# First tiles of a hybrid encoder trunk: order of fills, the inverse-root row read from its PSUM bank, no GpSimd in the first normalisation, one power op issued early

## The chip, the cores and the metric

The kernel runs on one core of a Trainium2 chip. The metric is the device time of one execution in microseconds. A core has five instruction queues, which each run their own list in order: PE (matrix multiplies), DVE (vector), ACT (scalar, activation functions), POOL (GpSimd) and SP, which here only issues DMA transfers. They wait for each other through semaphores, so an instruction that waits holds up everything behind it in its own queue.

## The reference

One layer of a hybrid streaming encoder is applied to a prompt of 2048 tokens and to a sample of 32 tokens, width 1024, all in float32. Cut to what matters here:

```
mod = (silu(c) @ ada_w + ada_b)            # 6 x 1024: shift, scale, gate of two norms
sh1, sc1, gt1, sh2, sc2, gt2 = split(mod)
h = rmsnorm(x) * g * (1 + sc1) + sh1       # rmsnorm(x) = x * rsqrt(mean(x*x) + 1e-6)
p = h @ w_in                               # u, v, q, k, v', z, a, b
a_out = u * (W_s rmsnorm(v) + b_s)         # spatial gating over 128 positions
b_out = rmsnorm(gated_delta_rule(q, k, v', a, b)) * silu(z)
x = x + gt1 * (concat(a_out, b_out) @ w_out)
h = rmsnorm(x) * g2 * (1 + sc2) + sh2
x = x + gt2 * (relu(h @ w_up)**2 @ w_down)
y = rmsnorm(x)
```

Besides `y`, the last convolution rows, the final delta-rule states and the normalised `v` rows of the sample are returned.

## The kernel before

Activations are held with the 1024 channels on partitions, as eight tiles `k` = 0 to 7 of 128 channels, and tokens along the free dimension. Tokens are worked in two halves (1024 and 1056), each cut into groups of 512, or of 384, 384 and 288. Every large product is split in three to keep float32 accuracy: operands are held as a high part and a remainder, `BH`/`BL` for activations and `wh`/`wl` for weights, and PE runs high x high, high x low, low x high. The high part is a copy on ACT, the remainder a subtraction on DVE.

The stages are: `startup` (first statistics, the first modulation and the first projection `z`, up to some 60 us), the mixers (`v_stage`, the delta rule and the `u_stage` of each half, to some 1014 us), and the feed-forward part to the end.

`startup` loads the eight tiles of group 0 (`load(0)`, names `s_477` to `s_480`, two tiles in each: `s_477` holds k = 0 and 1, `s_478` holds 2 and 3, and so on). ACT squares them, DVE adds the squares into `row[0]` (`s_493`), and `rms_row` sums over the partitions with PE (bank `M`, four columns), scales on DVE (`rcol`), raises to the power -1/2 on POOL (`tt` with `pow`, exponent `mhalf`), and spreads the result back over all partitions with four PE transposes into another bank `M`; ACT then copies that bank into `row[0]`. In between, `ada_first(k)` computes shift and scale of tile k: two loads of 512 KB (`ada`, four buffers `s_469` to `s_472`, SP waits for a free one), eight small PE products into a bank `C`, an ACT copy, two transposes back into that bank, four DVE additions into `modc` and one scaling (`a`). `h_tile` then makes the activation tile: `h_value` multiplies x by the row of inverse roots (on POOL where k % 3 == 2, so k = 2 and 5, otherwise on DVE), applies scale and shift (on POOL for k = 1 and 5, ACT for 3 and 7, DVE for the others), and `split` makes `BH[k]` and `BL[k]`. Twelve products follow for each k: four heads of `z`, three each, into three banks `g` and one bank `L`.

Group 1 of the first half takes the same way behind it (`load(1)`, `stats(1)`, with the additions alternating between DVE and POOL), while PE goes on to `v_stage`. `consts` loads constants and fills zeros on POOL: the delta-rule state, padding, and buffers whose upper part must be zero.

No queue order is written by hand. Each helper records its instruction in `Program` with an engine, an estimated cost and its predecessors; `Program.schedule` then plays the whole list through a model of the five engines (costs, latencies between engines, a shared port of DVE and POOL) and emits every queue in the order of the modelled starts. So an edit at the beginning can change the order everywhere behind it. The semaphore waits are set afterwards from the data that the instructions touch.

The helpers' lines: L351 `act`, L366 `tt`, L371 `stt`, L380 `ts`, L389 `cp`, L393 `fill`, L404 `dma`, L412 `mms` (all matrix products), L423 `tr` (transposes).

Of the kernel before, what the change touches and what calls it, by code (L numbers as in the profile page):

```python
# [11 lines left out]
ALU = mybir.AluOpType  # L12
# [31 lines left out]
PE, DVE, ACT, POOL, DMA, NONE = range(6)  # L44
# [23 lines left out]
def segs(hf, g):  # L68
    o, w = GROUPS[hf][g]
    if hf == 1 and g == 2:  # L70
        return [(0, w - NS, 0), (w - NS, NS, 1)]
    return [(0, w, 0)]
# [52 lines left out]
class View:  # L125
# [52 lines left out]
    def bc(self, shape):  # L178
        return self.step("broadcast_to", np.broadcast_to(np.uint8(0), shape), self.reg, list(shape))
# [15 lines left out]
def R(x):  # L195
    return x.ap if isinstance(x, View) else x
# [140 lines left out]
class Kern:  # L337
# [50 lines left out]
        e = self._e(eng)  # L388
        self.p.op(eng, c, lambda: e.tensor_copy(R(out), R(in_)), [out], [in_])  # L389

    def fill(self, out, value, eng=POOL):
        e = self._e(eng)
        self.p.op(eng, 100 + out.n, lambda: e.memset(R(out), value), [out], [])  # L393

    def transpose32(self, out, in_):
        nc = self.nc
# [261 lines left out]
    def startup(self):  # L658
        i, c = self.i, self.dma
        c(self.craw, i["cT"])  # L660
        self.act(self.cs, self.craw, AF.Silu)
        self.fill(self.ones, 1.0, DVE)
        self.fill(self.mhalf, -0.5, DVE)
        xr = [[8, 9, 10, 11], [4, 5, 7, 12]]
        x = [[self.slot(s, lo, (P, 512)) for s in xr[g] for lo in (0, HALF)] for g in range(2)]
        load = lambda g: [c(x[g][k], self.x_src(0)(k, 512 * g, 512)) for k in range(KT)]
        row = [self.row[:, 512 * g : 512 * g + 512] for g in range(2)]

        def stats(g):
            acc = row[g]  # L670
            self.act(acc, x[g][0], AF.Square)
            for k in range(1, KT):
                sq = self.half("E")
                self.act(sq, x[g][k], AF.Square)
                self.tt(acc, acc, sq, ALU.add, DVE if g == 0 or k % 2 else POOL)
            self.rms_row([acc], 512, acc)

        load(0)
        k1 = self.slot(13, 512, (P, 248))
        c(k1, i["k1"])  # L680
        self.adab = k1[:, :96].re("p (j k q) -> p j k q", j=6, k=KT)
        self.cp(self.nrm, k1[:, 96:120].re("p (n k) -> p n k", n=3))
        self.cp(self.ident, k1[:, 120:248])
        stats(0)
        self.sq = self.slab_list()
        self.sn = self.slab(*self.sq.pop(0))
        z = [self.next_slab(), self.sn]
        ps = [self.bank("C") for _ in range(2)]
        for e in range(2):
            self.fill(ps[e], 0.0, DVE)  # L690
        zs = [self.bank(t) for t in "gggL"]
        for k in range(KT):
            self.ada_first(k, ps[k % 2])
            self.h_tile(0, 0, k, x[0][k], row[0], self.a1, 0)
            for h in range(H):
                self.gemm_k(zs[h][:, :512], *z[h // 2], h % 2, 0, 0, k)
        for h in range(H):
            self.z_out(0, 0, h, zs[h])
        load(1)
        stats(1)  # L700
        for k in range(KT):
            self.h_tile(0, 1, k, x[1][k], row[1], self.a1, 0)
        self.next_slab()
        self.consts()

    def consts(self):
        i = self.i
        ld = lambda v, src: self.dma(v, src, 4 * int(np.prod(v.shape)))
        bc = lambda v, n: self.dma(v, i[n].partition_broadcast(P))
        with self.p.at(GEMM):  # L710
            ld(self.wsT, i["wsT"])
            self.fill(self.wsT[64:128, :, 0:64], 0.0)
            bc(self.sgub, "sgub")
            bc(self.sgug, "sgug")
            ld(self.triu, i["triu"])
            ld(self.mask, i["mask"])
            ld(self.convw, i["convw"])
            ld(self.sconv, i["sconv"])
            ld(self.dngc, i["dngc"])
            bc(self.dtb, "dtb")  # L720
            bc(self.alog, "alog")
            for h in range(H):
                self.fill(self.S[h], 0.0)
            self.fill(self.halo, 0.0)
            self.fill(self.ab, 0.0)
            zero = self.slot(4, 0, (P, 1024))[:36]
            self.fill(zero, 0.0)
            for d in self.ud_d:
                self.dma(d.re("c a x -> (c a) x"), zero)
            self.fill(self.z0, 0.0)  # L730

            for x in self.r1s + self.vns + self.ofs:
                self.fill(x, 0.0)
            zero = self.slot(4, 0, (P, 384))
            self.fill(zero, 0.0)
            for h in range(H):
                self.dma(self.us_d[h][1][:, 1024:], zero[:, :P])
                self.dma(self.pk_d[h][8][:, :, :P], zero.re("p (a b) -> p a b", a=3))
# [113 lines left out]
        self.tt(bl, x, bh.f32(), ALU.subtract, eng)  # L852

    def h_value(self, hf, g, k, x, r, a, kind):
        self.tt(x, x, r, ALU.mult, POOL if k % 3 == 2 else DVE)
        for so, sw, q in segs(hf, g):
            s = slice(so, so + sw)
            c, b = a[:, k, q : q + 1], self.modc[:, kind, k, q : q + 1]
            if k % 4 == 1 and not kind:
                self.ts(x[:, s], x[:, s], c, ALU.mult, b, ALU.add, POOL)  # L860
            elif kind or k % 4 == 3:
                self.act(x[:, s], x[:, s], AF.Identity, scale=c, bias=b)
            else:
                self.ts(x[:, s], x[:, s], c, ALU.mult, b, ALU.add)
# [1032 lines left out]
```

## Time and profile before

| what | value |
|---|---|
| median of 3 runs | 2337.24 us (2336.88 to 2339.47) |
| the profiled execution, its own time | 2330.84 us |
| its span | 2328.8 us |
| granted PE clock, mean | 0.998 |
| PE busy | 2292.2 us, 98% |
| DVE busy | 1653.2 us, 71% |
| ACT busy | 1226.1 us, 53% |
| POOL busy | 607.5 us, 26% |
| moved by DMA | 552.59 MB, 237 GB/s mean |

PE is busy nearly all the time, and its busy time is made of pipelined products. So what matters is where PE is not busy: 16.1 us of that lie in the first 60 us, 9.4 us in the last 25 us, and 11.0 us in the 2244 us between. A row of the timeline gives start, duration, engine, line, operation, output<-inputs, and in brackets the idle time before it with what ended it; of a row with xN, the start is that of the first and the duration that of all N together.

### The profile page before, as it was taken

How to read it: one execution, taken by the hardware profiler on the slowest of the kernel's cores; microseconds unless marked ns; L12 is line 12 of the kernel's file. 1: busy time of each engine (PE TensorE's matmuls, PEld its weight loads, DVE VectorE, ACT ScalarE, POOL GpSimd, SP SyncE). 2: the span in 40 equal slices, each digit the busy share in tenths (PEclk: the TensorE clock that was granted, in tenths of full speed). 3: DMA queues.
4: the chain of work that ended last, by engine and by line, in shares of the span. 5: the costliest groups of instructions: out<-in, count | busy, mean ns of one | idle time of the engine just before them, and what ended most of it. 6: DMA issues, size and time to landing. Idle time of an engine off the chain costs nothing.

```text
span 2328.8 us, 45703 instructions
## 1 busy us (share of the span) xinstructions
PE 2292.2 (98%) x15906; PEld 2171.0 (93%) x15906; DVE 1653.2 (71%) x3651; ACT 1226.1 (53%) x2816; POOL 607.5 (26%) x830
## 2 busy tenths in 40 slices
PE   7999999999999999999999999999999999999998
PEld 4877879999999888999999999999999999999998
DVE  5557646667655546589999989776668886666775
ACT  5465546666655435376556555753344564334343
POOL 2235331332423323345544424200000250000001
PEclk9999999999999999999999999999999999999999
DMA  9789666657557767888777786997667797666771
GB/s 322 224 291 317 222 183 214 188 166 232 165 157 225 242 204 232 262 290 277 248 255 251 256 280 229 344 321 233 221 214 252 264 302 232 221 214 215 246 225 54
DMA packets 367247, 552.59 MB, mean 237 GB/s; under 512 B 70988, under 2 KB 191200, under 8 KB 367016
## 3 DMA queue, kind: packets, MB, share of 16 engines
q1 hardware_dynamic: 367016, 549.68, 72.5%
q8 instruction: 125, 2.05, 0.4%
q14 instruction: 106, 0.87, 0.1%
HBM read 395.25 MB, written 154.28 MB: 236 GB/s over the span
## 4 chain that ended last, share of the span: by engine, by line
PE 59%; DMA 3%; DVE 2%; issue 1%; ACT 1%; POOL 0%; SPq 0%; POOLq 0%; DVEq 0%; ACTq 0%
PE f L412 52%; PE g L412 6%; DMA s<-th_d 1%; PE C L412 1%; DVE s L366 1%; DVE s L371 1%; ACT s L351 0%; DVE BL L366 0%; DMA wh<-sd_d 0%; DVE wl L366 0%; POOL s L366 0%; DMA wr<-w_o 0%; PE B L412 0%; DMA th_d<-s 0%; ACT BH L351 0%
## 5 line engine op out<-in xcount | busy, mean ns | idle before, releaser
L351 ACT ACTIVATE s<-s 128x348 fp32r<-128x348 f32 (+13 forms) x1077 | 496.0, 483 | 341.3 <-DVE s L366 131.4
L412 PE MATMUL f<-s,wh 128*128 128x348 f32 (+1 forms) x2768 | 662.4, 322 | 0.4 <-DVE s L366 0.3
L412 PEld LDWEIGHTS f<-s,wh 128*128 128x128 f32 x2768 | 481.0, 188 | 2.2 <-DVE s L366 1.9
L366 DVE TENSOR_TENSOR s<-f,s 128x348 f32<-128x348 f32 (+1 forms) x696 | 349.6, 515 | 170.4 <-PE f L412 169.2
L412 PE MATMUL f<-s,wl 128*128 128x348 f32 (+1 forms) x1384 | 444.9, 321 | 0.0
L412 PE MATMUL g<-BH,wh 128*128 128x512 f32 (+2 forms) x1112 | 411.3, 370 | 0.0
L412 PE MATMUL g<-BH,wl 128*128 128x512 f32 (+2 forms) x1112 | 391.4, 352 | 0.0
L412 PE MATMUL g<-BL,wh 128*128 128x512 f32 (+2 forms) x1112 | 390.1, 351 | 0.0
L366 DVE TENSOR_TENSOR s<-s,s 128x348 fp32r<-128x348 f32 (+7 forms) x679 | 350.9, 546 | 45.7 <-POOL s L366 16.7
L412 PE MATMUL f<-BL,wh 128*128 128x348 f32 (+1 forms) x1024 | 330.2, 322 | 0.0
L412 PE MATMUL f<-BH,wh 128*128 128x348 f32 (+1 forms) x1024 | 329.3, 322 | 0.0
L412 PE MATMUL f<-BH,wl 128*128 128x348 f32 (+1 forms) x1024 | 328.7, 321 | 0.0
L351 ACT ACTIVATE wh<-s 128x512 fp32r<-128x512 f32 (+1 forms) x277 | 173.7, 634 | 232.0 <-PE f L412 190.6
L366 POOL TENSOR_TENSOR s<-s,s 128x512 f32<-128x512 f32 (+5 forms) x156 | 197.6, 1275 | 330.5 <-ACT s L351 163.4
L366 POOL TENSOR_TENSOR s<-s 64x39 f32<-64x39 f32 (+12 forms) x298 | 159.5, 535 | 444.0 <-issue 381.7
L412 PEld LDWEIGHTS f<-s,wl 128*128 128x128 f32 x1384 | 260.6, 188 | 0.0
L366 DVE TENSOR_TENSOR wl<-s,wh 128x512 fp32r<-128x512 f32 (+1 forms) x277 | 215.4, 786 | 35.7 <-ACT wh L351 34.6
L412 PEld LDWEIGHTS g<-BH,wh 128*128 128x128 f32 x1112 | 209.6, 188 | 22.7 <-issue 5.2
L412 PEld LDWEIGHTS g<-BH,wl 128*128 128x128 f32 x1112 | 208.9, 188 | 19.1
L412 PEld LDWEIGHTS g<-BL,wh 128*128 128x128 f32 x1112 | 210.0, 189 | 16.7 <-DVE BL L366 0.2
L371 DVE SCALAR_TENSOR_TENSOR s<-s,s,s 128x256 f32<-128x256 f32 (+5 forms) x318 | 164.2, 538 | 59.4 <-ACT s L351 34.2
L366 DVE TENSOR_TENSOR wl<-wr,wh 128x512 fp32r<-128x512 f32 (+2 forms) x164 | 159.1, 973 | 57.5 <-ACT wh L351 54.9
(116 smaller groups left out, 3328.0 us busy)
## 6 DMA issues: line engine op xcount, KB each, us to landing
s<-w_u SPq DMA_DIRECT2D x124, 256.0 KB
s<-w_d SPq DMA_DIRECT2D x121, 256.0 KB
wh<-su_d SPq DMA_DIRECT2D x114, 256.0 KB
wl<-su_d SPq DMA_DIRECT2D x114, 256.0 KB
wh<-sd_d SPq DMA_DIRECT2D x100, 256.0 KB
wl<-sd_d SPq DMA_DIRECT2D x100, 256.0 KB
wr<-w_b SPq DMA_DIRECT2D x42, 512.0 KB
s<-adaw SPq DMA_DIRECT2D x32, 512.0 KB
```

What stands on the lines that cost most here:

```text
L351: self.p.op(ACT, c, lambda: nc.scalar.activation(out=R(out), in_=R(in_), func=func, **{k: R(v) for k, v in kw.items()}), [out, accum], [in ...
L366: self.p.op(eng, c, lambda: e.tensor_tensor(out=R(out), in0=R(a), in1=R(b), op=op), [out], [a, b])
L371: self.p.op(DVE, c, lambda: nc.vector.scalar_tensor_tensor(out=R(out), in0=R(a), scalar=R(s), in1=R(b), op0=op0, op1=op1), [out], [a, s, b])
L412: nc.tensor.matmul(R(out), R(l), R(r), **kw)
```

## The change

Four edits to the first tiles.

- `fill` can take predecessors, and the fills of `consts` now all name the last product of the first `z` (`end`) as one. This holds for the planner only: it plans them behind that product, and no semaphore wait comes of it.
- `rms_row` of group 0 is called without an output: the row stays in its PSUM bank and is not copied to `row[0]`; the eight multiplications of `h_value` read the bank.
- `h_value` does not use POOL for the multiplication where the row lies in a bank (`r.whole`), so k = 2 and 5 go to DVE.
- One more power op (`ones` to the power `mhalf`, into `rcol[1]`, 128x4) is recorded at the beginning on POOL.

```
-    def fill(self, out, value, eng=POOL):
+    def fill(self, out, value, eng=POOL, after=()):
         e = self._e(eng)
-        self.p.op(eng, 100 + out.n, lambda: e.memset(R(out), value), [out], [])
+        self.p.op(eng, 100 + out.n, lambda: e.memset(R(out), value), [out], [], after=after)
...
         self.fill(self.mhalf, -0.5, DVE)
+        self.tt(self.rcol[1], self.ones[:, :4], self.mhalf, ALU.pow, POOL)
...
-            self.rms_row([acc], 512, acc)
+            return self.rms_row([acc], 512, acc if g else None)
...
-        stats(0)
+        r = stats(0)
...
-            self.h_tile(0, 0, k, x[0][k], row[0], self.a1, 0)
+            self.h_tile(0, 0, k, x[0][k], r, self.a1, 0)
             for h in range(H):
                 self.gemm_k(zs[h][:, :512], *z[h // 2], h % 2, 0, 0, k)
+        end = (len(self.p.ops) - 1,)
...
-        self.consts()
-
-    def consts(self):
+        self.consts(end)
+
+    def consts(self, after):
         i = self.i
+        fill = lambda v, x: self.fill(v, x, after=after)
...
-            self.fill(self.wsT[64:128, :, 0:64], 0.0)
+            fill(self.wsT[64:128, :, 0:64], 0.0)
...
-        self.tt(x, x, r, ALU.mult, POOL if k % 3 == 2 else DVE)
+        self.tt(x, x, r, ALU.mult, POOL if k % 3 == 2 and not r.whole else DVE)
```

All other fills of `consts` change from `self.fill` to `fill` in the same way.

What the queues look like, at three places. First DVE, from the first modulation to the first remainder tile. `C_503` and `C_504` are the banks of the modulation, `s_482` its bias, `s_493` the row of inverse roots in SBUF, `a_89` the scale, `BL_79` the remainder of tile 0, `wr_96` raw weights. Before:

```order
L366 TENSOR_TENSOR modc<-C_503,s_482 128x2x2
L366 TENSOR_TENSOR s_477<-s_477,s_493 128x512
L366 TENSOR_TENSOR modc<-C_503,modc 128x2x2 x3
L380 TENSOR_SCALAR a_89<-modc,nrm 128x2
L380 TENSOR_SCALAR s_477<-s_477,a_89,modc 128x512
L366 TENSOR_TENSOR modc<-C_504,s_482 128x2x2
L366 TENSOR_TENSOR s_477<-s_477,s_493 128x512
L366 TENSOR_TENSOR modc<-C_504,modc 128x2x2
L366 TENSOR_TENSOR s_478<-s_478,s_493 128x512
L366 TENSOR_TENSOR BL_79<-s_477,BH_71 128x512
L366 TENSOR_TENSOR wl<-wr_96,wh 128x1024
```

The same place on DVE now, from the fourth multiplication on (three multiplications and three additions to `modc`, one by one in turn, stand ahead of it); `M_555` is the bank with the row.

```order
L366 TENSOR_TENSOR s_478<-s_478,M_555 128x512
L366 TENSOR_TENSOR modc<-C_503,modc 128x2x2
L366 TENSOR_TENSOR s_479<-s_479,M_555 128x512
L380 TENSOR_SCALAR a_89<-modc,nrm 128x2
L366 TENSOR_TENSOR s_479<-s_479,M_555 128x512
L380 TENSOR_SCALAR s_477<-s_477,a_89,modc 128x512
L366 TENSOR_TENSOR modc<-C_504,s_482 128x2x2
L366 TENSOR_TENSOR s_480<-s_480,M_555 128x512
L366 TENSOR_TENSOR modc<-C_504,modc 128x2x2
L366 TENSOR_TENSOR s_480<-s_480,M_555 128x512
L366 TENSOR_TENSOR wl<-wr_96,wh 128x1024
L366 TENSOR_TENSOR BL_79<-s_477,BH_71 128x512
```

Six multiplications instead of one now stand ahead of the scaling of tile 0, and the remainder `BL_79` has moved from ahead of the weight remainder `wl` to behind it and behind all eight multiplications.

Then PE at the first products of `z`; `g_505` is the bank of head 0, and the line `C_503<-ident` is the transposes of the modulation of k = 2. Before:

```order
L412 MATMUL C_503<-s_469,s_486 2x256 x4
L412 MATMUL C_503<-s_470,s_486 2x256 x4
L412 MATMUL g_505<-BH_71,wh 128x512
L412 MATMUL g_505<-BL_79,wh 128x512
L412 MATMUL g_505<-BH_71,wl 128x512
L412 MATMUL g_506<-BH_71,wh 128x512
L412 MATMUL g_506<-BL_79,wh 128x512
L412 MATMUL g_506<-BH_71,wl 128x512
L423 MATMUL C_503<-ident,s_482 128x128 x2
```

And PE now:

```order
L412 MATMUL C_503<-s_469,s_486 2x256 x4
L412 MATMUL C_503<-s_470,s_486 2x256 x4
L423 MATMUL C_503<-ident,s_482 128x128 x2
L412 MATMUL g_505<-BH_71,wh 128x512
L412 MATMUL g_505<-BL_79,wh 128x512
L412 MATMUL g_505<-BH_71,wl 128x512
L412 MATMUL C_504<-s_471,s_486 2x256 x4
L412 MATMUL C_504<-s_472,s_486 2x256 x4
```

The transposes of k = 2 have moved from behind six products to ahead of the first one.

Last POOL, around the power of the second row (`rcol_95<-rcol_95,mhalf`); `s_484` is `wsT`, whose fill waits for its load, and `s_493` is here the sum of squares of group 1. Before:

```order
L366 TENSOR_TENSOR s_493<-s_493,s_491 128x512
L366 TENSOR_TENSOR s_493<-s_493,s_492 128x512
L366 TENSOR_TENSOR s_493<-s_493,s_490 128x512
L393 MEMSET s_484 64x4x64
L366 TENSOR_TENSOR rcol_95<-rcol_95,mhalf 128x4
```

POOL now:

```order
L366 TENSOR_TENSOR s_493<-s_493,s_490 128x512
L393 MEMSET s_486 128x136
L393 MEMSET s_484 64x4x64
L393 MEMSET s_486 128x36
L393 MEMSET s_482 128x128 x2
L366 TENSOR_TENSOR rcol_95<-rcol_95,mhalf 128x4
```

Of the fills that left the beginning of the queue, four now stand between the last addition and the second power, three of them behind the fill of `wsT`. Behind these places the order of all queues differs up to the first part of the feed-forward stage; PE has the same 14272 products in both, and ACT one table load fewer.

More of the change, by code (lines that the diff above doesn't have):

```diff
@@ L722, in consts @@
             for h in range(H):
-                self.fill(self.S[h], 0.0)
-            self.fill(self.halo, 0.0)
-            self.fill(self.ab, 0.0)
+                fill(self.S[h], 0.0)
+            fill(self.halo, 0.0)
+            fill(self.ab, 0.0)
             zero = self.slot(4, 0, (P, 1024))[:36]
-            self.fill(zero, 0.0)
+            fill(zero, 0.0)
             for d in self.ud_d:
                 self.dma(d.re("c a x -> (c a) x"), zero)
-            self.fill(self.z0, 0.0)
+            fill(self.z0, 0.0)
             for x in self.r1s + self.vns + self.ofs:
-                self.fill(x, 0.0)
+                fill(x, 0.0)
             zero = self.slot(4, 0, (P, 384))
-            self.fill(zero, 0.0)
+            fill(zero, 0.0)
             for h in range(H):
```

## The prediction

> **What bounds the kernel.** I read the page first, then the busy time by stage, then the timeline of the first 60 us, where the edits lie. The sum and PE's row of the page, and one row for each stage (columns: stretch, its length, busy time of PE, PEld, DVE, ACT, POOL, clock, DMA share, GB/s):
>
> ```profile
> span 2328.8 us, 45703 instructions
> PE 2292.2 (98%) x15906; PEld 2171.0 (93%) x15906; DVE 1653.2 (71%) x3651; ACT 1226.1 (53%) x2816; POOL 607.5 (26%) x830
> ...
> 0.00:60.00 60.00, 43.86 (x281) 26.90 (x282) 34.92 (x84) 30.67 (x49) 14.85 (x25) 1.00 0.90 317
> 60.00:1014.00 954.00, 945.05 (x7440) 845.55 (x7438) 579.23 (x1596) 521.10 (x1370) 309.83 (x589) 1.00 0.71 224
> 1014.00:2304.00 1290.00, 1287.95 (x8088) 1283.87 (x8089) 1024.13 (x1939) 669.01 (x1388) 277.87 (x212) 1.00 0.74 246
> ```
>
> PE bounds the kernel. From 60 to 2304 us it stands idle for 8.95 + 2.05 = 11.0 us only; in the first 60 us for 16.1, of which 12.4 pass before its first instruction. The change leaves PE's work alone. It can move the end in two ways: through when PE gets past the first tiles, and through how much PE waits in the new order behind them.
>
> The start, in order of time:
>
> ```profile
> 0.72 0.84 POOL L393 MEMSET s<- 128x136 f32 x6 [0.29 <-POOLq L1890]
> ...
> 12.41 1.87 PE L412 MATMUL M<-ones,s 128*128 128x1 f32 x8 [12.41 <-DVE s L366]
> 14.20 1.89 PE L412 MATMUL C<-s,s 128*2 128x256 f32 x16
> 14.55 1.93 POOL L366 TENSOR_TENSOR rcol<-rcol,mhalf 128x4 f32<-128x4 f32 x1 [12.99 <-DVE rcol L380]
> 16.54 1.12 PE L423 MATMUL M<-ident,rcol 128*128 128x128 f32 x4 [0.45 <-POOL rcol L366]
> 17.69 0.60 ACT L351 ACTIVATE s<-M 128x512 f32<-128x512 f32 x1 [1.15 <-PE M L423]
> 18.32 0.69 DVE L366 TENSOR_TENSOR s<-s,s 128x512 f32<-128x512 f32 x1
> 18.37 3.00 POOL L366 TENSOR_TENSOR s<-s,s 128x512 f32<-128x512 f32 x2 [1.88 <-ACT s L351]
> 18.93 0.55 DVE L366 TENSOR_TENSOR modc<-C,modc 128x4 f32<-128x4 f32 x3
> 19.51 0.65 DVE L380 TENSOR_SCALAR a<-modc,nrm 128x2 f32<-128x2 f32 x1
> 20.20 1.45 DVE L380 TENSOR_SCALAR s<-s,a,modc 128x512 f32<-128x512 f32 x1
> 21.57 0.15 DVE L366 TENSOR_TENSOR modc<-C,s 128x4 f32<-128x4 f32 x1
> 21.64 0.67 DVE L366 TENSOR_TENSOR s<-s,s 128x512 f32<-128x512 f32 x1
> 21.68 0.63 ACT L351 ACTIVATE BH<-s 128x512 fp32r<-128x512 f32 x1 [1.33 <-DVE s L380]
> 22.22 1.04 ACT L351 ACTIVATE wh<-wr 128x1024 fp32r<-128x1024 f32 x1
> 22.76 0.61 PE L412 MATMUL C<-s,s 128*2 128x256 f32 x8 [1.37 <-DMA s<-ada]
> 22.91 0.68 DVE L366 TENSOR_TENSOR BL<-s,BH 128x512 fp32r<-128x512 f32 x1
> 23.30 0.50 PE L412 MATMUL g<-BH,wh 128*128 128x512 f32 x1
> 23.50 0.38 ACT L351 ACTIVATE s<-C 128x256 f32<-128x256 f32 x1 [0.24 <-PE C L412]
> 23.52 1.21 DVE L366 TENSOR_TENSOR wl<-wr,wh 128x1024 fp32r<-128x1024 f32 x1
> 23.65 0.50 PE L412 MATMUL g<-BL,wh 128*128 128x512 f32 x1
> 24.65 0.15 DVE L366 TENSOR_TENSOR modc<-C,modc 128x4 f32<-128x4 f32 x1
> ...
> 27.71 0.55 DVE L380 TENSOR_SCALAR s<-s,a,modc 128x512 f32<-128x512 f32 x1
> ```
>
> The reader is to see two things here. While POOL multiplies (18.37 to 21.37), the DVE scaling takes 1.45 us instead of the 0.55 of 27.71, and the small one before it 0.65. And the first product, at 23.30, comes behind a modulation product that waited for a load until 22.76.
>
> **The change, part by part.**
>
> *Early power.* The first power takes 1.93 us, the second (57.86, shown below) 1.03. With one issued early, I take 1.03 for the first too: ready at 15.6 instead of 16.5. But PE is in its modulation products until 14.20 + 1.89 = 16.09, so the transposes come forward by no more than PE's own wait, 0.45.
>
> *Row read in its bank.* The ACT copy (0.60) goes. The transposes end at 16.09 + 1.12 = 17.21, and DVE can multiply from 17.25 instead of 18.32, 1.07 us earlier. The price of a multiplication with a bank as operand is shown elsewhere in the kernel:
>
> ```profile
> L366 DVE TENSOR_TENSOR s<-s,s 128x512 f32<-128x512 f32 x23 | 15.7, 687 | 10.3 <-POOL s L366 5.2 <-ACT s L351 4.6
> ...
> L366 DVE TENSOR_TENSOR s<-M,s 128x512 f32<-128x512 f32 x16 | 11.0, 688 | 5.7 <-PE M L412 5.6
> ```
>
> 688 against 687 ns: nothing for the eight. [...]
>
> *GpSimd left out, and the order that comes of it.* Two POOL multiplications (3.00 us) go, and the DVE scaling falls back from 1.45 to 0.55. But six multiplications now stand ahead of it. From start to start one takes 0.61 (18.32 to 18.93), a `modc` addition between two of them 0.07 (21.57 to 21.64), and I take 0.13 for `a`. Six, four and one: 3.66 + 0.28 + 0.13 = 4.07, so the scaling starts at 17.25 + 4.07 = 21.3 and ends at 21.9, where it ended at 21.65. What the start gained is spent. `BH` of tile 0 now also stands behind `wh` on ACT. That `wh` waits for its load, which lies just ahead of the one that landed by 22.76; its 0.52 MB take 1.65 us at the 317 GB/s of this stretch, so it lands about 21.1, `wh` ends about 22.2 and `BH` 0.63 later, at 22.8. `BL` stands behind two more multiplications and additions (21.8 + 1.36 = 23.2) and behind `wl` (start to start 24.65 - 23.52 = 1.13): it runs from 24.3 to 25.0, where it ended at 23.59. The second product so starts at 25.05 instead of 23.65: PE is **1.4 us later**. The transposes of k = 2 now stand ahead of the first product and wait for the copy of the bank (done about 23.85); that lies inside the same wait. Since they (some 0.2) are then already done, PE is some 1.2 us behind at this point.
>
> *What this costs at the end of the first tiles.* Three later waits decide it:
>
> ```profile
> 38.40 0.61 PE L412 MATMUL C<-s,s 128*2 128x256 f32 x8 [0.48 <-DMA s<-ada]
> ...
> 49.97 2.65 ACT L351 ACTIVATE s<-s 128x512 f32<-128x512 f32 x4 [1.73 <-DMA s<-xT]
> 54.16 0.69 DVE L366 TENSOR_TENSOR s<-s,s 128x512 f32<-128x512 f32 x1 [1.47 <-POOL s L366]
> 55.00 1.02 PE L412 MATMUL M<-ones,s 128*128 128x1 f32 x8 [0.68 <-DVE s L366]
> 57.31 0.31 POOL L393 MEMSET s<- 64x256 f32 x1 [3.18 <-DMA s<-wsT]
> 57.56 0.16 DVE L380 TENSOR_SCALAR rcol<-M 128x4 f32<-128x4 f32 x1
> 57.86 1.03 POOL L366 TENSOR_TENSOR rcol<-rcol,mhalf 128x4 f32<-128x4 f32 x1 [0.25 <-DMA s<-dtb]
> 58.94 0.65 PE L423 MATMUL M<-ident,rcol 128*128 128x128 f32 x4
> ```
>
> At 38.40 PE waits for a load of the modulation (at least the 0.48 shown), and the transfers run near their rate up to there, so a late PE catches up by that much: 0.7 is left of 1.2. At 55.00 PE waits 0.68 for the sum of squares of group 1, whose last squares wait for loads at 49.97: this swallows the rest. And at 58.94 PE takes up the second power. Its input at 57.56 comes behind two weight remainders on DVE that do not depend on this change, so it can't be much earlier, however early PE arrives. Now three more fills, behind that of `wsT`, stand ahead of that power (six take 0.84 at 0.72): 57.31 + 0.31 + 3 x 0.14 is 58.0 instead of 57.86. So PE passes this point at about 59.1 instead of 58.94: **+0.1 us**. The bounds are -0.7 (the wait at 55.00 goes, and nothing takes its place) and +1.4 (nothing is absorbed); I take +0.1, since the power is nearest to the point where it ends.
>
> *Fills.* At the beginning, 0.84 us of fills on POOL covered nothing anybody waited for (POOL waited 12.99 us for `rcol`); the later place costs what is counted above. The fills have no wait of their own for the `z` products. On SP, one load of x moves ahead of a small load that waits for PE; it lies behind the wait of 49.97 and can only help there. One ACT table load goes; ACT is 53% busy, so nothing.
>
> *The new order behind.* The same products run in another order up to the feed-forward part. The 11.0 us of idle PE bound it above: nothing can be gained beyond that. For a loss I take the same size, a doubling. Without a row that says which, I take 0.
>
> **Sum.** 2330.84 (the profiled execution: 2328.8 span and 2.0 around it) + 0.1 + 0 = 2330.9. The median of the runs shown is 6.4 above that execution; on that scale the forecast is 2337.24 + 0.1 = **2337.3 us**, no change. A difference under 0.2% (4.7 us) is about what a measurement of this kernel can't tell from none.
>
> **The rivals.** The delta rule's chain decides most of them. One row of PE's weight-load side, between 60 and 1100 us, and one of the DVE updates that it waits for:
>
> ```profile
> PEld C L412 <- DVE s L371: 7.1, 19, 0.7
> ...
> L371 DVE SCALAR_TENSOR_TENSOR s<-s,s,C 128x128 f32<-128x128 f32 x68 | 20.5, 344 | 29.2 <-PE C L412 29.2
> ```
>
> - *Faster: the chain's products come later in PE's queue than now.* PE waits at 19 places for the state update of the chain. If the new order puts other products ahead of each, up to 7.1 us come back: 2337.3 - 7.1 = 2330.2. For it: those waits are real. Against: the planner uses the same latencies as before.
> - *Slower: they come earlier.* There are 68 such updates, and a wait is 7.1 / 19 = 0.37 us. If 22 more of the 68 wait, 22 x 0.37 = 8.1 us are added: 2345.4. It decides from 13 more on (4.7 / 0.37). For it: PE takes its queue in order, so each such wait is paid in full. Against: only 19 of 68 wait now, in an order of the same planner.
> - *The start gains.* The wait of 0.68 at 55.00 goes and the power of row 2 comes earlier too: 2337.24 - 0.7 = 2336.5, still no change.
> - *The change doesn't help because nothing absorbs the late `BL`:* 2337.24 + 1.4 = 2338.6, no change.
>
> **How the numbers follow.** No change as worked out 0.42, the start's gain 0.08, its loss 0.10, the faster chain 0.20, the slower one 0.20. So faster 0.20, same 0.60, slower 0.20. The first three lie within 2335 to 2340. To leave out no more than 2 in 10, the range takes in half of each chain rival: 2331 to 2344.
>
> **What would show it.** Right: the first transposes into `M` start near 16.1; no ACT copy behind them; the first scaling on DVE takes 0.55 and ends near 21.9; `BL` of tile 0 ends near 25; the second row's transposes on PE start within 0.3 of 58.94; idle PE from 60 to 2304 near 11 us. Wrong: a second product before 24, PE past the second transposes by 58, or idle PE in the mixers under 5 or over 15 us. The forecast fails if those waits move by more than 4.7 us, or if the load waited for at 22.76 and 38.40 comes at another time than now.

## The result: slower by 16.6 us

| | kernel before | changed kernel |
|---|---|---|
| median of 5 runs each | 2337.51 us (2336.88 to 2339.47) | 2354.12 us (2351.33 to 2356.77) |
| ratio, 95% interval | 1 | 1.0066 (1.0054 to 1.0079) |
| the profiled execution, its own time | 2330.84 us | 2356.77 us |
| mean granted PE clock in it | 0.998 | 0.995 |

The two profiled executions lie 25.9 us apart, the medians 16.6: the profiled one of before is the fastest on record of it, that of after the slowest of its five. Where this matters, a second profile with the order of the kernel before is used beside it (the first experiment).

The stages after, in the columns of the prediction's first fence:

```profile
PE 2302.0 (98%) x15906; PEld 2175.6 (92%) x15906; DVE 1656.5 (70%) x3653; ACT 1223.5 (52%) x2814; POOL 600.9 (26%) x829
```

```profile
0.00:60.00 60.00, 43.69 (x277) 26.93 (x277) 35.97 (x87) 29.95 (x48) 12.36 (x21) 0.97 0.91 321
60.00:1014.00 954.00, 935.14 (x7329) 833.08 (x7327) 567.24 (x1570) 509.43 (x1347) 301.31 (x587) 0.99 0.69 217
1014.00:2304.00 1290.00, 1282.84 (x8048) 1276.09 (x8047) 1027.54 (x1944) 667.22 (x1385) 275.72 (x210) 1.00 0.76 251
```

PE has the same 15906 instructions in both profiles, and yet its busy time grew by 9.8 us; a lower clock in places and a larger number of waits, both shown below, are a part of that. Its idle time from 60 to 2304 us grew from 11.0 to 18.9 + 7.2 = 26.0 us. The first 60 us are as they were (16.3 us idle, before 16.1).

The start after, to be laid beside the timeline in the prediction:

```profile
1.09 1.01 POOL L366 TENSOR_TENSOR rcol<-ones,mhalf 128x4 f32<-128x4 f32 x1 [0.65 <-DVE mhalf L393]
...
14.10 1.22 DVE L366 TENSOR_TENSOR wl<-wr,wh 128x1024 fp32r<-128x1024 f32 x1
14.26 1.94 POOL L366 TENSOR_TENSOR rcol<-rcol,mhalf 128x4 f32<-128x4 f32 x1 [12.16 <-DVE rcol L380]
...
16.25 1.12 PE L423 MATMUL M<-ident,rcol 128*128 128x128 f32 x4 [0.44 <-POOL rcol L366]
...
21.41 0.54 DVE L380 TENSOR_SCALAR s<-s,a,modc 128x512 f32<-128x512 f32 x1
...
22.73 0.61 ACT L351 ACTIVATE BH<-s 128x512 fp32r<-128x512 f32 x1
23.06 0.61 PE L412 MATMUL C<-s,s 128*2 128x256 f32 x8 [1.84 <-DMA s<-ada]
...
24.33 0.68 DVE L366 TENSOR_TENSOR BL<-s,BH 128x512 fp32r<-128x512 f32 x1
24.58 0.78 PE L412 MATMUL g<-BH,wh 128*128 128x512 f32 x1
25.16 0.71 PE L412 MATMUL g<-BL,wh 128*128 128x512 f32 x1
...
58.51 1.01 POOL L366 TENSOR_TENSOR rcol<-rcol,mhalf 128x4 f32<-128x4 f32 x1 [1.52 <-DVE rcol L380]
59.58 0.65 PE L423 MATMUL M<-ident,rcol 128*128 128x128 f32 x4 [0.84 <-POOL rcol L366]
```

But for the first power and `BH`, this is the start that the prediction drew, step by step. The time went behind it.

### The profile page after: what moved, and what is told of

The parts are those of the page before. It is cut to its first block, busy times and chain, and to the rows that moved or that the text cites. A ratio compares the mean times of both kernels' runs of the same rounds, so it can differ in the third digit from the quotient of the medians.

```text
span 2354.3 us, 45695 instructions
## 1 busy us (share of the span) xinstructions
PE 2302.0 (98%) x15906; PEld 2175.6 (92%) x15906; DVE 1656.5 (70%) x3653; ACT 1223.5 (52%) x2814; POOL 600.9 (26%) x829
## 4 chain that ended last, share of the span: by engine, by line
PE 44%; DVE 4%; DMA 2%; issue 1%; ACT 1%; POOL 0%; SPq 0%; POOLq 0%; DVEq 0%; ACTq 0%
PE f L412 44%; DVE s L366 3%; DVE wl L366 1%; ACT s L351 1%; DMA s<-th_d 1%; POOL s L366 0%; DVE s L371 0%; DMA sd_d<-wh 0%; DMA th_d<-s 0%; DMA s<-x_d 0%; ACT wh L351 0%; DMA su_d<-s 0%; DMA su_d<-wl 0%; DMA wl<-sd_d 0%; ACT BH L351 0%
## 5 line engine op out<-in xcount | busy, mean ns | idle before, releaser
L366 DVE TENSOR_TENSOR s<-s,s 128x348 fp32r<-128x348 f32 (+8 forms) x673 | 346.5, 543 | 55.9 <-ACT s L351 24.2
L366 POOL TENSOR_TENSOR s<-s,s 128x512 f32<-128x512 f32 (+5 forms) x154 | 189.3, 1236 | 317.2 <-ACT s L351 149.5
L371 DVE SCALAR_TENSOR_TENSOR s<-s,s,s 128x128 f32<-128x128 f32 (+5 forms) x318 | 163.7, 536 | 58.9 <-ACT s L351 39.6
L351 ACT ACTIVATE wh<-wr 128x512 fp32r<-128x512 f32 (+2 forms) x164 | 130.2, 795 | 128.4 <-PE f L412 55.2
```

The lines of the kernel that those rows point to most:

```text
L351: self.p.op(ACT, c, lambda: nc.scalar.activation(out=R(out), in_=R(in_), func=func, **{k: R(v) for k, v in kw.items()}), [out, accum], [in ...
L366: self.p.op(eng, c, lambda: e.tensor_tensor(out=R(out), in0=R(a), in1=R(b), op=op), [out], [a, b])
L371: self.p.op(DVE, c, lambda: nc.vector.scalar_tensor_tensor(out=R(out), in0=R(a), scalar=R(s), in1=R(b), op0=op0, op1=op1), [out], [a, s, b])
```

## The experiments

Theory: the four edits and the first tiles cost nothing; the 16.6 us come from the order that the planner drew for everything behind them. Rivals: the edits themselves or the start (A), both (B), and several on single places, named where they are tested. Each run is given as a ratio to the kernel before on the same chip. Its median there was 2338.6 us for e1 to e4, 2341.2 for e5 to e8 and 2341.4 for e9 to e12, so medians of different sets are not compared.

### The order of one kernel behind the start of the other (e1, e2)

A kernel can hold both plans: `ordered` builds the program with and without the edits, plans both, keeps the first 60 us of its own plan and puts the rest in the other plan's order. Of the planner's blocks of work some 40 stand elsewhere in the start, and behind it some 1400 on PE and DVE together and 1300 on ACT, POOL and SP together. For e1:

```
+EDITS = {'fills', 'pool', 'power', 'bank'}
+OTHER = set()
+CUTS = (60000, 0)
...
+    head = [o for o in mine if o.start < lo]
+    rest = [o for o in mine if o.start >= lo]
+    key = {id(o): (at[id(o)], n) for n, o in enumerate(rest)}
+    rest.sort(key=lambda o: key[id(o)])
...
-            for o in self.p.schedule():
+            for o in ordered(self):
                 o.fn()
```

and for e2 the two sets are exchanged.

> All four edits are in, and the work of the first 60 us of the plan stands in the order of the changed kernel; everything behind stands on each engine in the order that the kernel before has there. Theory (the first tiles come out even, and the 16.6 us lie in the new order behind them): 2337, within 2 us, and no stretch of half clock at 378 to 389 us. Rival A (the start itself costs it: the fills that are placed later, or the scalings and powers in other places of their queues): 2354. Rival B (both halves cost some): 2341 to 2350.

> The reverse: none of the four edits is in and the first 60 us of the plan are those of the kernel before, but everything behind stands in the order of the changed kernel. Theory: 2354, within 3 us, with TensorE idle near 377 and its clock at 0.50 for some 10 us behind. Rival A: 2337. Rival B: 2341 to 2350.

Measured: e1 2339.82 us, ratio 1.0004 (0.9994 to 1.0013); e2 2356.62 us, 1.0072 (1.0055 to 1.0089). All four edits with the old order behind them cost nothing; no edit at all with the new order behind costs all of it. That shows theory against A and B.

Where the order loses it is read from the busy time by stretch. First e1, with the edits and the old order, then the changed kernel. The profile of e1 is that of its fastest execution and the other that of the slowest of the changed kernel, so their spans lie 20.4 us apart (2333.9 and 2354.3), where the ratios, 1.0004 and 1.0066, make it 14.5:

```profile
60.00:240.00 180.00, 178.08 (x1071) 143.36 (x1072) 107.32 (x230) 102.59 (x209) 63.47 (x88) 1.00 0.84 276
240.00:370.00 130.00, 128.84 (x1017) 105.11 (x1015) 76.39 (x171) 72.55 (x185) 38.18 (x94) 1.00 0.67 211
370.00:400.00 30.00, 30.00 (x266) 29.20 (x257) 19.31 (x79) 20.47 (x75) 6.03 (x9) 1.00 0.60 196
400.00:560.00 160.00, 156.59 (x1508) 149.04 (x1507) 109.77 (x379) 99.56 (x295) 52.38 (x138) 1.00 0.61 186
560.00:850.00 290.00, 288.03 (x2630) 267.83 (x2629) 167.38 (x520) 152.66 (x445) 91.55 (x216) 1.00 0.66 202
850.00:1014.00 164.00, 160.95 (x956) 149.69 (x955) 97.81 (x215) 72.87 (x163) 56.90 (x51) 1.00 0.79 250
1014.00:2320.00 1306.00, 1302.76 (x8183) 1297.90 (x8182) 1040.01 (x1966) 675.55 (x1400) 283.94 (x217) 1.00 0.74 245
```

```profile
60.00:240.00 180.00, 174.82 (x1040) 138.44 (x1038) 104.00 (x218) 94.98 (x189) 63.61 (x84) 1.00 0.81 262
240.00:370.00 130.00, 130.00 (x831) 106.41 (x830) 72.17 (x162) 69.56 (x171) 39.62 (x94) 1.00 0.64 207
370.00:400.00 30.00, 26.04 (x370) 23.56 (x369) 16.44 (x51) 17.97 (x69) 4.11 (x6) 0.83 0.45 135
400.00:560.00 160.00, 156.75 (x1516) 149.32 (x1515) 108.72 (x366) 99.51 (x292) 50.04 (x133) 1.00 0.62 190
560.00:850.00 290.00, 284.21 (x2615) 265.03 (x2614) 172.99 (x552) 159.14 (x470) 88.64 (x221) 1.00 0.66 202
850.00:1014.00 164.00, 163.31 (x972) 150.33 (x970) 92.92 (x222) 68.26 (x161) 55.29 (x51) 1.00 0.76 244
1014.00:2320.00 1306.00, 1298.84 (x8149) 1292.09 (x8148) 1035.69 (x1959) 676.39 (x1404) 278.50 (x213) 1.00 0.75 248
```

Idle PE in the mixers is 11.5 us in e1 and 18.9 in the changed kernel: 7.4 more, of which 3.3 lie before 240 us, 4.0 at 370 to 400, 3.8 at 560 to 850, while -1.2 and -2.4 come back at 240 to 370 and 850 to 1014. At 370 to 400 the clock is also down to 0.83. The feed-forward stage has 3.9 more idle time, of which more below.

### Fills and early power alone (e3)

`bank` and `pool` are left out, `fills` and `power` stay:

```
+EDITS = {'fills', 'power'}
```

> Two of the four edits alone: the fills behind the first z products and the early power; the row of inverse roots is still copied and GpSimd keeps its two multiplies. On TensorE, VectorE, ScalarE and SyncE the order is then the one of the kernel before. Theory: 2337.3, within 1 us, since these two move nothing but GpSimd's own instructions. Rival A in the form that the late fills hold up what reads them: 2340 to 2354.

Measured: 2338.46 us, 0.9997 (0.9985 to 1.0009), as the theory has it. So the other pair, the row read in its bank and the multiplications taken off POOL, is what made the planner draw another order.

### The place at 375 to 390 us (e4, e5, e6)

PE in the changed kernel:

```profile
374.73 0.28 PE L412 MATMUL g<-wl,BH 128*128 128x260 f32 x1
377.04 1.13 PE L412 MATMUL L<-s 128*128 128x256 f32 x4 [2.03 <-ACT s L351]
379.38 0.66 PE L423 MATMUL L<-ident,s 128*128 128x128 f32 x2 [1.21 <-issue]
380.76 1.12 PE L423 MATMUL L<-ident,s 128*128 128x128 f32 x4 [0.72 <-ACT s L351]
381.53 0.56 PE L412 MATMUL g<-wh,BH 128*128 128x260 f32 x1
```

The large products stop at 374.73 and go on at 381.53. The clock of it, in stretches of 1 us (the third number from the end):

```profile
378.00:379.00 1.00, 0.17 (x1) 0.00 (x0) 0.75 (x3) 0.61 (x2) 0.00 (x0) 0.91 0.02 5
379.00:380.00 1.00, 0.62 (x2) 0.29 (x2) 1.00 (x3) 0.00 (x0) 0.00 (x0) 0.50 0.28 43
...
388.00:389.00 1.00, 1.00 (x7) 1.00 (x7) 0.00 (x0) 0.95 (x4) 0.00 (x0) 0.50 0.03 8
389.00:390.00 1.00, 1.00 (x9) 1.00 (x9) 0.16 (x1) 0.99 (x3) 0.00 (x0) 0.97 0.00 0
```

No wait is longer than 2.03 us, and the clock stands at 0.50 until 389, 8 us after the last of them. And ACT, with the copies of the weight slab through its one staging buffer (`wh<-wr`):

```profile
365.38 1.28 ACT L351 ACT_TABLE_LOAD   x1 [1.11 <-issue]
366.68 1.06 ACT L351 ACTIVATE s<-s 128x1024 f32<-128x1024 f32 x1
367.76 1.28 ACT L351 ACT_TABLE_LOAD   x1
...
369.33 1.06 ACT L351 ACTIVATE wh<-wr 128x1040 fp32r<-128x1040 f32 x1
...
376.88 1.06 ACT L351 ACTIVATE wh<-wr 128x1040 fp32r<-128x1040 f32 x1
```

An exponential with a table load on either side (3.6 us) stands ahead of the slab's third copy; in the kernel before it stood ahead of the second, 20 us earlier. My reading was that this delays the slab and so leaves PE without products. e4 moves that one instruction. The numbers in the diffs of e4 to e6 count the recorded blocks: 2085 is the exponential, 3071 to 3073 are the third copy, its subtraction and the next load, 3074 and 3075 the fourth copy and subtraction, 2137 to 2154 the local blocks that wait.

```
+MOVES = [(2085, 3071)]
...
+    for i, j in MOVES:
+        out.remove(ops[i])
+        out.insert(out.index(ops[j]) + 1, ops[i])
```

> The changed kernel with one ScalarE instruction moved: the exponential of 128x1024 that stands at 366.68 us with a table load on either side goes behind the third copy of the slab's halves through the one staging buffer (369.33), so that this copy, and the load, the copy and the subtraction that follow it, come some 3.6 us earlier. Theory (TensorE stands at 374.7 to 381.5 for want of this slab, 4.0 us idle in three waits, and its clock then falls to 0.50 for some 9 us, which costs another 4.5): 2345 to 2347, with the granted clock at 1.00 throughout 370 to 395. Rival C (the clock plays no part, only the waits do): 2350. Rival D (the waits come from the local products' own chain on ScalarE and only change place): 2354.

Measured: 2353.85 us, 1.0071 (1.0049 to 1.0092): no gain. The copy did come earlier, but the subtraction that frees the buffer did not. In e4, whose earlier times run some 3 us behind:

```profile
373.19 0.61 DVE L371 SCALAR_TENSOR_TENSOR s<-L,s,s 128x128 f32<-128x128 f32 x2
373.72 1.23 DVE L366 TENSOR_TENSOR wl<-wr,wh 128x1040 fp32r<-128x1040 f32 x1
```

Two updates that need the exponential stand ahead of it on DVE. The copy now ran at 369.26, and the subtraction waited 3.4 us for its turn. The time is the one that rival D gave, but PE's three waits did not change place as rival D says: they are the same, of 2.07, 1.21 and 0.71 us. e6 moves the whole chain on all engines, and 13 products ahead of the local blocks:

```
+    for i, j in ((3072, 3071), (3073, 3072), (2085, 3073), (3074, 2115), (3075, 3074)):
+        out.remove(ops[i])
+        out.insert(out.index(ops[j]) + 1, ops[i])
...
+        d = 6 if i in (2137, 2138) else 10 if i in (2143, 2144) else max(0, 13 - c // 4)
+        last = max(last, c + d)
+        rows.append((last, o))
```

> The changed kernel with the place at 366 to 390 us mended in the order of all engines concerned: the third copy of the weight slab through the staging buffer, its subtraction and the next load go ahead of the 128x1024 exponential and its table loads; the fourth copy and subtraction go ahead of eight other ScalarE and VectorE instructions; and 13 of the next products stand on TensorE ahead of the local blocks that wait, a lead that is given back over the next 50 products. Theory: idle and half clock both go, the product at 401 us comes 1 to 4 us late against the kernel before and not 11, and the median is 2344 to 2347. Rival D (ScalarE, busy without a gap from 369 to 378, is the bound there, so that the wait only changes its place): 2352 to 2355, with the same idle time between 370 and 400 us under other names.

Measured: 2361.31 us, 1.0088 (1.0067 to 1.0110): not faster, and by the middle of the interval 5 us slower than the changed kernel. ACT and PE in e6:

```profile
375.44 1.07 ACT L351 ACTIVATE wh<-wr 128x1040 fp32r<-128x1040 f32 x1 [2.09 <-DMA wr<-w_v]
...
382.44 1.13 PE L412 MATMUL L<-s 128*128 128x256 f32 x4 [3.41 <-ACT s L351]
```

Now ACT waits 2.09 us for the slab's last load with everything queued behind it, and PE runs out of products ahead of the local block and waits 3.41. The wait changed its place, as rival D had it, though by a load that ACT waits for and not because ACT is busy throughout, and the time lies above rival D's too. Two repairs by hand failed, so this place is shown to cost time, and not shown to be cheap to mend.

e5 asks only what the lower clock costs. It leaves the order and puts matmuls into the waits whose results nobody reads:

```
+IDLE_WORK = [(2137, 14), (2143, 8), (2151, 4)]
...
+                k.nc.tensor.matmul(R(ps), R(x[:, 0:128]), R(x[:, 0:WZ]), start=True, stop=True, skip_group_check=True)
```

> The changed kernel in its own order, with 26 matmuls added that compute nothing which is used (128x260 products of two pieces of BH into the bank that the next product overwrites): 14 ahead of the local products that wait at 374.7 us, 8 ahead of the transposes that wait at 378.4, 4 ahead of those at 380.3. The waits of 2.0, 1.2 and 0.7 us stay, but TensorE has work in them. Theory (the near-idle stretch makes the granted clock fall to 0.50, and products at half rate cost some 4.5 us of the 16.6): the clock stays at 1.00 from 378 to 395, and the product that comes 11 us late at 401 comes 6 to 7 us late; the median falls to 2349 or 2350. Rival C (the clock falls for another reason, or the slow products wait for something else): clock 0.50 as before, 2354.

Measured: 2350.89 us, 1.0044 (1.0030 to 1.0058). The same place in e5:

```profile
375.00:380.00 5.00, 4.41 (x33) 3.92 (x32) 2.11 (x10) 4.04 (x16) 1.01 (x1) 1.00 0.61 175
380.00:385.00 5.00, 4.76 (x155) 4.23 (x154) 3.12 (x11) 2.51 (x11) 1.01 (x1) 1.00 0.74 234
385.00:390.00 5.00, 5.00 (x87) 4.42 (x89) 1.82 (x9) 3.49 (x10) 0.28 (x1) 1.00 0.10 34
```

The clock stays at 1.00, and the product that came at 401.38 comes at 398.24, though e5 reached the place 0.37 us later (its last large product ahead of the waits starts at 375.10, and not at 374.73). So useless work in a wait made the kernel faster: 3.5 us at this place by the trace, 0.0022 of the time (5 us, with intervals that overlap a little) by the medians. Rival C falls. The bound worked out from the rows was 4.0 us (8.0 us at half rate); I had expected 4.5.

### Half of the new order (e9, e10)

The same merge as in e1, with the cut at 340 us (e9) and at 480 us (e10). For e9:

```
+CUTS = (340000, 0)
```

> All four edits; the order of the changed kernel for the first 340 us of its plan (the two transfers that TensorE waits for at 218 and 228 us lie in it, 1.7 and 1.4 us in the profile), and behind that the order of the kernel before. Theory (a sum of places): the place at 375 to 390 us is gone, the waits at 218 and 228 stay: 3 to 5 us above the kernel before, ratio 1.0013 to 1.0021. Rival F (the loss lies in what follows 480 us): ratio 1.000 to 1.001.

> The same with the order of the changed kernel for the first 480 us of its plan, so with the place at 375 to 390 us: its 4.0 us of idle TensorE and its half clock, which was worth 3.2 us at the product at 401 us when TensorE had work in the gap. Theory: 7 to 9 us more than the one to 340, ratio 1.0045 to 1.006, and the clock at 0.50 from 380 to 389. Rival F: within 2 us of the one to 340.

Measured: e9 2353.90 us, 1.0053 (1.0036 to 1.0070); e10 2361.54 us, 1.0089 (1.0066 to 1.0111). e10 lies 0.0036, 8.4 us, above e9 as expected, but both lie above their own forecasts. The trace of e9 says why:

```profile
368.08 0.69 PE L423 MATMUL L<-ident,s 128*128 128x128 f32 x2 [7.88 <-DVE s L371]
```

The seam between two orders made a wait of its own. e10 has one too (4.36 us at 519), so that the 8.4 us are not clean either. What holds is that behind the seam e9 keeps its distance to the kernel before for some 310 us: PE's 3000th and 6000th instructions (at 448.0 and 759.2 us before) both start 19.4 us later. And ahead of the seam PE has 5.3 us idle from 60 to 240 us, before 0.7. So in this stretch the old order loses nothing. Behind it the distance grows to 24.5 us at the 12000th instruction (1700.7 us before); e1, with the same order there, goes from 1.3 to 3.8.

### Other orders with no edit, and with all of them (e7, e8, e11, e12)

Two constants of the planner's model, changed by a little, draw other orders for both kernels:

```
-TURN = 84
+TURN = 78
```

```
-LATENCY = {(PE, DVE): 230, (PE, ACT): 230, (PE, POOL): 230, (DVE, PE): 380, (DVE, DVE): 130, (DVE, ACT): 160,
+LATENCY = {(PE, DVE): 230, (PE, ACT): 235, (PE, POOL): 230, (DVE, PE): 380, (DVE, DVE): 130, (DVE, ACT): 160,
```

> The kernel before with one constant of its planner changed: what a turn from small blocks to large products is held to cost, 78 in place of 84. No work is changed; behind 60 us of the plan some 500 TensorE blocks, 750 VectorE and 500 ScalarE and SyncE instructions stand in another order. Theory (an order drawn anew behind the start moves the time by several us, whatever draws it, and the order of the kernel before is a good one): 2342 to 2356. Rival E (orders of this planner are worth the same within 2 us, and the edits themselves make the order worse): 2336 to 2340.

> The changed kernel, all four edits, with the same constant at 78. Theory: again another order, so that its distance to the kernel before with 78 need not be +16.6 and may have the other sign; 2336 to 2356. Rival E: 2354, and 16 us above the kernel before with 78.

> The kernel before with another constant of its planner changed: the time from a TensorE product to ScalarE is put at 235 ns in place of 230. No work is changed; some 290 blocks on TensorE stand in another order. Theory (an order drawn anew): 1.000 to 1.006 times the kernel before. Rival E: within 2 us of it.

> The changed kernel, all four edits, with the same constant at 235. Theory: its distance to the kernel before with 235 is another than +16.6, of either sign, 0.996 to 1.006 times that kernel. Rival E (the edits cost it by whatever order): 16 us above it, as with 230.

| planner's constants | without the edits | with the four edits | the edits cost |
|---|---|---|---|
| as they are | 1 | 1.0066 (1.0054 to 1.0079) | +0.66% |
| turn 78 | 1.0020 (1.0006 to 1.0034) | 1.0016 (1.0002 to 1.0030) | -0.04% |
| PE to ACT 235 | 1.0009 (0.9996 to 1.0022) | 0.9995 (0.9984 to 1.0006) | -0.14% |

With either constant the same edits cost nothing that can be told from zero. Rival E, by which they make every order worse, falls. None of the five other orders beats the kernel before; the theory's guess that an order drawn anew moves the time by several us is borne out once at its lower end (e7) and not clearly in e11. No version here is faster than both kernels.

## Why the prediction was wrong

*What bounds the kernel* held: PE, and the time can move only by the first tiles or by what PE waits for behind them.

*Early power* was wrong in its size and cost nothing. The first power on the row still took 1.94 us with one issued ahead of it. It runs beside the 1.22 us subtraction `wl` on DVE; the early one, while DVE fills banks, and the one at 58.51, with DVE at rest, took 1.01. So in these rows the length goes with that subtraction beside it and not with being the first. The transposes started at 16.25, for 16.1 forecast.

*Row read in its bank* was right. The eight multiplications form this row:

```profile
L366 DVE TENSOR_TENSOR s<-s,M 128x512 f32<-128x512 f32 x8 | 5.4, 676 | 2.1 <-PE M L423 2.1
```

676 ns each, where the prediction took 688.

*GpSimd left out* was right where it counts: scaling 0.54 us, ending at 21.95 (21.9); `BL` from 24.33 to 25.01 (24.3 to 25.0); second product at 25.16 (25.05). `BH` came later than forecast, and it cost nothing: the `wh` ahead of it waited for its load until 21.77 (21.1), so `BH` ended at 23.34 (22.8), still well ahead of `BL`.

*The end of the first tiles* was right in its sum. The second row's transposes came at 59.58, 0.64 after those of before, where I had allowed 0.3 (and the forecast's own 59.1 is nearly 0.2 after 58.94, not 0.1); but with unchanged or changed starts they came at 60.5, 61.7 and 62.0 in e1, e3 and e2, so one execution can't tell that. e1 settles it: the whole start is worth 0.04% (-0.06 to +0.13), forecast 0.1 us. The fills are in that sum. The table load is not: e1 has 40, as the kernel before, and the changed kernel 39.

*The new order behind* is the step that failed. It said that the 11.0 us of idle PE bound it, and took 0. Idle time says about what can be gained; it bounds no loss, and "a doubling" had no row behind it. The runs show a loss of 0.66%, all of it behind the start (e1, e2). What it consists of can be counted in the profiles of e1 and of the changed kernel, from the start of one PE instruction to that of the next, behind 60 us. Of the 20.4 us between them, 11.8 are more idle time (the 7.4 and 3.9 of the tables, and the edges of the stretches), and 3.9 are products at half clock, which no idle time counts. Another 4.1 us stand ahead of the waits: a 128x260 product is counted busy for 0.28 us, while the next can start 0.12 us behind it (374.61, 374.73), so that every wait costs more than the idle time shown, and there are 62 waits in place of 43. For the last two the prediction had no term. Not all of this is the order's: the feed-forward part's 3.9 us aren't shown to be, since e9, with the old order there, has more idle time there too (6.3 us from 1020 to 2000 us; before 1.7), and the two profiles are the ends of their spreads. Why the new order has more waits is followed at one place only. My sign for a wrong forecast, idle PE in the mixers over 15 us, is what came: 18.9.

*The rivals.* The slower one named the chain's updates, with 22 more waits. Both chain rivals took the price from PE's weight-load side, 7.1 us at 19 places. PE itself waited for these updates less, in the mixers before:

```profile
PE C L412 <- DVE s L371: 2.1, 8, 0.3
```

So some 2.1 us of idle time could have come back and not 7.1, and a wait is some 0.26 us and not 0.37. The longest waits of PE in the mixers after:

```profile
PE C L412 <- DVE s L371: 4.1, 10, 0.8
PE L L412 <- ACT s L351: 2.3, 2, 2.0
PE B L412 <- DMA s<-adaw: 1.7, 1, 1.7
PE L L423 <- DMA s<-kq_d: 1.4, 1, 1.4
```

The chain's grew from 2.3 us in e1 to 4.1, a small part. The next are local blocks behind ACT and two transfers, which the prediction didn't look at; the rest is spread over a dozen others of 1.2 us and less. A re-planned order has no single mechanism to price, so a chance of 0.60 on "same" was too sure: more of it should have been given to a wide loss.

## What to carry to other kernels

Where a planner orders the queues, an edit at one place is two changes: the edit, and a new draw of every order behind it. Measure them apart by giving the edited program the old order, before anything is concluded on the edit; here that turned +0.66% into 0. And idle time of the bounding engine says about how much can be won, never how much can be lost.

## What the runs showed of the hardware

*The clock falls around short waits.* In the changed kernel PE has waits of 2.03, 1.21 and 0.72 us within 5.8 us (375.01 to 380.76), and the granted clock is 0.50 for 10.2 us, from 378.81 to 389.05. One of the 128x260 products starts every 0.22 us there (387.26, 387.48), and every 0.12 us ahead of the waits (374.61, 374.73). From the beginning of the first wait to the fall PE is busy for 1.14 us of 3.81:

```profile
375.00:378.81 3.81, 1.14 (x5) 0.68 (x4) 1.27 (x8) 3.58 (x13) 1.01 (x1) 1.00 0.63 180
378.81:389.05 10.24, 8.95 (x157) 8.05 (x158) 4.04 (x14) 4.49 (x17) 1.01 (x1) 0.50 0.44 130
```

With matmuls put into the same waits (e5) PE is busy for 14.18 of the 15 us from 375 to 390, and the clock stays at 1.00. So at this place the fall goes with how little PE does, and not with what it waits for. How little it takes, and over what time, is not shown. Nor is what brings the clock back: PE is busy without a gap from 381.53 on (7.52 us), and the clock rises only at 389.05, 8 us after the last wait.

The same happened between 22 and 30 us in e1, e2 and e3, with either start, around a wait of PE for a load (1.52, 1.56 and 2.04 us; mean clock 0.76 from 16 to 30 us in each), and for 3.4 us in the changed kernel (0.50 from 23.83 to 27.24, behind a wait of 1.84 us); of all profiles here only that of the kernel before, the fastest execution, kept 1.00 throughout its first 60 us.

*The power op on POOL* (128x4) took 1.94 us beside a DVE subtraction of two SBUF operands (14.26 in the changed kernel), and 1.01 with DVE at rest (58.51) or filling banks (1.09).
